# Norm factor moved behind the transposes: x is turned and split as it is, and the factor is applied to results and to a second pair of parts

## The chip, the core and the metric

One core of one Trainium2 chip runs the whole program. Its engines are TensorE (PE, with its weight loads as PEld), VectorE (DVE), ScalarE (ACT), GpSimd (POOL) and SyncE (SP, which here only issues DMAs). Each runs its own queue in order and waits on semaphores for the others. The metric is the device time of one execution in microseconds (us), the median of several runs. All times below are us unless marked ns.

## What is computed

A decoder trunk of two layers on 256 tokens of 1024 channels, in float32. Each layer has a mixer and a stage of experts, and each begins with an RMS norm:

```python
def rms_norm(x, g):
    y = x * lax.rsqrt(jnp.mean(x * x, axis=-1, keepdims=True) + EPS)
    return y * g

for layer in range(2):
    h = rms_norm(x, norm1_g[layer])
    dq, dk, dv, fq, fk, fv, ff, ga, gb = split(h @ w_in[layer])
    y_diff = diff_attention(dq, dk, dv, ...)          # 4 heads, softmax minus lambda softmax
    y_fox = forgetting_attention(fq, fk, fv, ff + b)  # 8 heads
    x = x + (sigmoid(ga) * (y_diff @ w_diff_o) + sigmoid(gb) * (y_fox @ w_fox_o)) @ w_out
    t = rms_norm(x, norm2_g[layer])
    s = product_keys(t @ w_query)                     # two top-16 of 128, then top 16 of their sums
    experts, gates = select(s)                        # softmax over the 16 best of each head
    x = x + sum(gates * gelu(t @ expert_u[experts]) * expert_v[experts])
return rms_norm(x, final_norm_g)
```

The norm is one factor per token (a row of x), times one gain per channel. All 16384 experts are computed densely, and a dense gate picks among them.

## The kernel before

Every product runs in three passes on PE. A float operand is split into a rounded part (`hi`) and the rest (`lo`), and hi by hi, hi by lo and lo by hi are added up in PSUM (`mm3`, `rows_b`). The activations' two parts are `hT[0]` and `hT[1]`, turned: channels on the partitions, in eight blocks k of 128, by 256 tokens.

Weights come as a list of blocks of 512 KB in a fixed order (`plan`): 8 of wV, 32 of wA, 8 of wO, 8 of w_out, 16 of wQ, 128 of uT and 128 of v in each layer. SP fetches a block into one of three buffers; ACT copies it rounded to `hi`, and DVE subtracts to get `lo` (lines 92 and 93), with three buffers of each. `weights` hands out block n and first calls `ahead(n + 3)`, so the instructions that split blocks n + 1 and n + 2 stand in the queues of ACT and DVE ahead of what the caller issues next. The order of the program is the order of each engine's queue (`manual_schedule`); nothing is reordered later.

Where a stage ends, `sum_b` adds products of rows into four PSUM banks (two halves of the tokens by two halves of the channels, `PIECES`). The last two blocks (`TAIL`) are kept back and run piece by piece, so that the pieces are done one after the other. `norm_t` follows: `inv_rms` adds each piece to x (DVE, line 210), squares it (ACT, line 216) and gets the factor by a power on POOL and a Newton step on DVE. A diagonal of factors is made for each half of the tokens, and PE multiplies blocks of x by it (line 248), which turns and scales x at once. ACT and DVE then write the two parts with the gain (lines 253 and 254).

In the mixer eight value blocks follow (wV, 18 matmuls each: two halves of the tokens, three passes, three column groups of 344). Between them stand small steps: the layer's constants and, behind the fourth block, two table loads of ACT (lines 386 and 387). Then come 32 projections on wA (`proj`, 24 matmuls of 256 columns each) with attention between them. In the experts' stage 16 projections on wQ give the queries; behind each stands the score product of the one before (`score`, which reads the copy `q`). Then 48 projections on uT run while DVE selects the experts: `select` is a generator whose items are placed into slots j = -13 to 47 by a budget of 1.35 for each slot (`PIECE_US`, the yields are its costs, None ends a slot). Behind slot 47 the generator is run to its end, the first one-hots are made (lines 749 and 751), and after one more projection PE makes the first dense gate from them (line 760).

## Time and profile before

| | |
|---|---|
| median of 3 runs | 2009.3 us (2009.29 to 2009.52) |
| the profiled execution | 2009.3 us, its span 2007.5 us |
| PE, PEld | 1992.8 us (99%), 1833.4 us (91%) |
| DVE, ACT, POOL | 1412.1 us (70%), 1058.8 us (53%), 27.4 us (1%) |
| PE's granted clock | 0.999 of full speed |
| DMA | 351.96 MB, 175 GB/s |

The page gives each engine's busy time and the chain of work that ended last, followed back from the last instruction. The views behind it list waits by engine and line, instructions in order of time with the idle time before each in brackets, groups of instructions by their shapes, and stretches of the span. PE's matmuls overlap: one that is listed with 0.40 us may be followed by the next after 0.23, so distances between starts are what PE takes.

### The profile page before, as it was taken

The page shows a single profiled execution, that of the slowest core. Times are in us where ns is not written, and L with a number is a line of the kernel's source. Part 1 is how long each engine was busy: PE and PEld are TensorE (multiplying, and loading weights), DVE is VectorE, ACT ScalarE, POOL GpSimd, SP SyncE. Part 2 cuts the span into 40 slices and gives each one's busy share as a digit, 9 for nine tenths or more (in the row PEclk, how much of TensorE's full clock was granted, in tenths as well). Part 3 has the DMA queues.
Part 4 walks back from the last instruction along what each step waited for, and adds up shares of the span by engine and source line. Part 5 has one row for each costly group of instructions (what it writes and reads, how often), then busy time and mean ns, then how long its engine had stood idle before and what let it go on. Part 6 is the DMA issues. An engine that isn't in the chain of part 4 may idle for free.

```text
span 2007.5 us, 35728 instructions
## 1 busy us (share of the span) xinstructions
PE 1992.8 (99%) x14042; PEld 1833.4 (91%) x14042; DVE 1412.1 (70%) x2867; ACT 1058.8 (53%) x1954; POOL 27.4 (1%) x49
## 2 busy tenths in 40 slices
PE   9999999999999999999999999999999999999998
PEld 8998999999999888888899989999999998888886
DVE  5667798788888555555566677987888885555555
ACT  6665556554444444444466655465444444444444
POOL 2000000000000000000010000000000000000000
PEclk9999999999999999999999999999999999999999
DMA  6445555555555555555554455565555555555554
GB/s 226 149 157 168 161 180 181 187 164 163 158 168 167 190 189 189 189 189 189 189 167 148 148 180 159 190 180 179 167 159 161 167 174 188 189 189 189 189 188 153
DMA packets 97451, 351.96 MB, mean 175 GB/s; under 512 B 11473, under 2 KB 11510, under 8 KB 97281
## 3 DMA queue, kind: packets, MB, share of 16 engines
q1 hardware_dynamic: 95040, 345.09, 54.5%
q0 software_dynamic: 1664, 3.53, 0.6%
q8 instruction: 110, 1.80, 0.4%
q10 hardware_dynamic: 576, 1.05, 0.1%
q14 instruction: 61, 0.49, 0.1%
HBM read 348.56 MB, written 1.71 MB: 174 GB/s over the span
## 4 chain that ended last, share of the span: by engine, by line
PE 99%; DVE 0%; DMA 0%; issue 0%; ACT 0%; POOL 0%; SPq 0%; ACTq 0%; DVEq 0%
PE acc L154 39%; PE ps L121 17%; PE ps L122 17%; PE ps L123 17%; PE acc L760 3%; PE ps L154 1%; PE acc L783 1%; PE acc L248 1%; PE acc L627 1%; PE ps L557 0%; PE acc L569 0%; PE acc L644 0%; DMA x<-x 0%; PE acc L122 0%; PE acc L123 0%
## 5 line engine op out<-in xcount | busy, mean ns | idle before, releaser
L93 DVE TENSOR_TENSOR lo<-raw,hi 128x1024 fp32r<-128x1024 f32 (+1 forms) x656 | 801.7, 1224 | 500.2 <-ACT hi L92 498.2
L92 ACT ACTIVATE hi<-raw 128x1024 fp32r<-128x1024 f32 (+1 forms) x656 | 694.4, 1059 | 396.3 <-PE acc L154 389.2
L121 PE MATMUL ps<-hT,hi 128*128 128x256 f32 x2784 | 794.6, 285 | 0.0
L122 PE MATMUL ps<-hT,hi 128*128 128x256 f32 x2784 | 784.6, 282 | 0.0
L123 PE MATMUL ps<-hT,lo 128*128 128x256 f32 x2784 | 778.9, 280 | 0.0
L154 PE MATMUL acc<-hi,cut 128*128 128x512 f32 x2048 | 561.1, 395 | 0.0
L121 PEld LDWEIGHTS ps<-hT,hi 128*128 128x128 f32 x2784 | 523.0, 188 | 3.9 <-issue 3.7
L123 PEld LDWEIGHTS ps<-hT,lo 128*128 128x128 f32 x2784 | 524.9, 189 | 0.0
L122 PEld LDWEIGHTS ps<-hT,hi 128*128 128x128 f32 x2784 | 523.4, 188 | 0.3
L154 PEld LDWEIGHTS acc<-hi,cut 128*128 128x128 f32 x2048 | 385.4, 188 | 90.0
L154 PE MATMUL acc<-lo,cut 128*128 128x512 f32 x1024 | 321.9, 394 | 0.0
L154 PEld LDWEIGHTS acc<-lo,cut 128*128 128x128 f32 x1024 | 192.4, 188 | 45.8
L730 ACT ACTIVATE g<-ps 128x8 f32<-128x8 f32 (+31 forms) x158 | 44.5, 282 | 265.3 <-PE ps L123 260.7
L675 ACT ACTIVATE bufa<-ps 128x256 f32<-128x256 f32 x96 | 36.9, 384 | 115.5 <-PE ps L123 115.5
L751 DVE TENSOR_TENSOR ohG<-oh,tT 128x2048 f16<-128x2048 f16 x64 | 78.4, 1225 | 2.2
L749 DVE TENSOR_TENSOR oh<-iotax,tT 128x2048 f16<-128x2048 f16 x64 | 77.8, 1216 | 0.0
L760 PE MATMUL acc<-ohG,oh 128*128 128x128 f16 x1024 | 70.0, 219 | 0.0
L701 DVE TENSOR_TENSOR cut<-bufb,cut 128x256 fp32r<-128x256 f32 x160 | 67.1, 419 | 0.0
L700 ACT ACTIVATE cut<-bufb 128x256 fp32r<-128x256 f32 x160 | 64.0, 400 | 0.0
L760 PEld LDWEIGHTS <-oh 128*128 128x128 f16 x1024 | 58.9, 97 | 2.9
L734 DVE TENSOR_TENSOR bufb<-bufb,g 128x8 f32<-128x8 f32 (+31 forms) x158 | 46.1, 292 | 15.3 <-ACT g L730 15.3
L772 DVE SCALAR_TENSOR_TENSOR bufa<-acc,bufa 128x192 f32<-128x192 f32 x128 | 44.8, 350 | 0.0
(231 smaller groups left out, 1383.9 us busy)
## 6 DMA issues: line engine op xcount, KB each, us to landing
raw<-uT SPq DMA_DIRECT2D x256, 512.0 KB, 3.7
raw<-expert_v SPq DMA_DIRECT2D x256, 512.0 KB, 3.6
raw<-wA SPq DMA_DIRECT2D x64, 512.0 KB, 3.6
raw<-wQ SPq DMA_DIRECT2D x32, 512.0 KB, 3.6
raw<-wV SPq DMA_DIRECT2D x16, 516.0 KB, 4.0
raw<-wO SPq DMA_DIRECT2D x16, 512.0 KB, 3.6
raw<-w_out SPq DMA_DIRECT2D x16, 512.0 KB, 4.4
tb<-table POOLq DMA_DIRECT2D x2, 640.0 KB, 6.1
```

What stands on the lines that cost most here:

```text
L92: nc.scalar.activation(hi[:, :w], raw[:, :w], AF.Copy)
L93: nc.vector.tensor_sub(lo[:, :w], raw[:, :w], hi[:, :w].bitcast(F32))
L121: self.nc.tensor.matmul(ps, ah, bh, start=first and q == 0, stop=False)
L122: self.nc.tensor.matmul(ps, ah, bl, start=False, stop=False)
L123: self.nc.tensor.matmul(ps, al, bh, start=False, stop=last and q == n - 1)
L154: self.nc.tensor.matmul(ps[:, :width], a, b[:, g * width:(g + 1) * width], start=first and n == 0, stop=last and n == 2)
L700: nc.scalar.activation(a[:, 0], chunk(n), AF.Copy)
L701: nc.vector.tensor_sub(a[:, 1], chunk(n), a[:, 0].bitcast(F32))
L734: nc.vector.tensor_mul(chunk(J)[:, :t0], chunk(J)[:, :t0], g[:, :t0])
L749: nc.vector.tensor_tensor(flat(oh), self.iotax.rearrange("p n t -> p (n t)")[:, None].to_broadcast([128, TB, 256]), cols[0][:, :, None].to ...
L751: nc.vector.tensor_tensor(flat(og), flat(oh)[:, None, TB * 128:].to_broadcast([128, 2, TB * 128]), cols[1][:, :, None].to_broadcast([128, ...
L760: self.nc.tensor.matmul(banks[t // 4][:, t % 4], oh[:, 0, t // 2, :, t % 2], og[:, k, t // 2, :, t % 2], start=k == 0, stop=k == 1)
```

## The change

`norm_t` is gone. Instead x is turned by PE transposes without the factor and split with the gain alone, a piece at a time (`tip`: four transposes of a piece and four ACT evictions; `turn_lo`: the DVE part). `sum_b` takes a target `turn` and puts the first three pieces' steps between its own last matmuls; the fourth (`turn_last`) stands inside the first product of the next stage. For layer 0's start three tips run at once.

The factor is computed beside the next stage by `scaled`, a generator of eight steps: squares, power, factor and diagonal, a product of a matrix of ones with the diagonals that spreads the factor over the partitions, and four steps that make a second pair of parts, two blocks k each (two DVE operations, an ACT copy, a DVE subtraction).

- Mixer: the value products use the unscaled `hT`; their results are scaled as they leave PSUM. The wA projections use the scaled pair `hs`. `scaled` takes one step behind each value block, two behind the seventh and eighth.
- Experts: `hs` holds the unscaled pair, on which all 16 query projections run; the factor enters the Exp of the gates. The scaled pair is written to `hT`, for uT. `scaled` takes steps in slots -15 to -12 and in -10, -8, -6 and -4; in these last four the selection gets no items.
- The first two query projections have an order of their own (`proj_first`): passes before blocks k.
- At the start all four x transfers go by SP's queue, and the identity by ACT's in place of POOL's.
- The order of k becomes 0 to 7, value banks are others, and `hs` lives in a pool that is opened for each layer and closed after the selection.

```diff
-KO = [0, 2, 4, 6, 1, 3, 5, 7]
+KO = list(range(KT))
...
+    def proj_first(self, h, *key, turn=False):
+
+        w = self.by_k(self.weights(*key))
+        ps = self.bank("ps")[:, :S]
+        lo, up = range(4), range(4, KT)
+        if turn:
+            order = [(0, 0, lo), None, (1, 0, lo), (0, 0, up), (1, 0, up), (0, 1, KO)]
+        else:
+            order = [(0, 0, KO), (0, 1, KO), (1, 0, KO)]
+        for n, o in enumerate(order):
+            if o is None:
+                self.turn_last()
+                continue
+            for k in o[2]:
+                self.nc.tensor.matmul(ps, w[o[0]][:, k], h[o[1]][:, k], start=n == 0 and k == 0,
+                                      stop=n == len(order) - 1 and k == KT - 1)
         return ps
...
-    def sum_b(self, n, key, lhs_of):
+    def sum_b(self, n, key, lhs_of, turn=None):
...
+        if turn:
+            self.turn_begin(*turn, [acc[1][0], acc[1][1]])
+        for p, (tt, c, width) in enumerate(PIECES):
             ps = acc[tt][c // 512][:, c % 512:c % 512 + width]
-            for lhs, w, j in late:
-                self.rows_b([ps], lhs, [p[:, c:] for p in w], tt, width, False, j == n - 1)
+            for m, (lhs, w, j) in enumerate(late):
+                last = turn and p == 3 and m == TAIL - 1
+                for n in range(3):
+                    if last and n == 2:
+                        self.tip(2)
+                    a = lhs[n // 2][..., tt * 128:(tt + 1) * 128]
+                    self.nc.tensor.matmul(ps, a, w[n % 2][:, c:c + width], start=False, stop=j == n_all and n == 2)
+                if turn and p == 2 and m == 0:
+                    self.tip(1)
+                    self.turn_lo(0, range(2))
             self.late.append(ps)
+            if turn:
+                if p < 3:
+                    self.add(p)
+                if p == 1:
+                    self.tip(0)
+                if p == 2:
+                    self.turn_lo(0, range(2, 4))
+                    self.turn_lo(1, range(2))
+                if p == 3:
+                    self.add(3)
+                    self.turn_lo(1, range(2, 4))
+                    self.turn_lo(2, range(4))
...
+    def tip(self, n):
...
+        for k in range(4):
+            nc.tensor.transpose(banks[n][:, k * 128:(k + 1) * 128],
+                                self.x[:, tt, c + k * 128:c + (k + 1) * 128], self.ident)
+        for k in range(4):
+            q = c // 128 + k
+            nc.scalar.activation(h[0][:, q, tt * 128:(tt + 1) * 128], banks[n][:, k * 128:(k + 1) * 128], AF.Copy,
+                                 scale=g[:, q:q + 1])
...
+    def turn_lo(self, n, ks):
...
+            self.nc.vector.scalar_tensor_tensor(h[1][:, q, tt * 128:(tt + 1) * 128], banks[n][:, k * 128:(k + 1) * 128],
+                                                g[:, q:q + 1], hv, op0=OP.mult, op1=OP.subtract)
...
+    def turn_last(self):
+        self.tip(3)
+        self.turn_lo(3, range(4))
+
+    def scaled(self, pool, h, out, rs):
...
+        for tt in range(2):
...
+            nc.scalar.activation(junk, self.x[:, tt], AF.Square, scale=1.0 / 32, accum_out=ss[:, tt:tt + 1])
+        yield
...
+        vy = self.rsqrt_begin(pool, v)
+        yield
...
+        for tt in range(2):
+            nc.vector.tensor_scalar(diag[:, tt], self.ident, rs[:, tt:tt + 1], None, op0=OP.mult)
+        yield
+        ps = self.bank("acc")[:, :S]
+        nc.tensor.matmul(ps, self.ones, diag.rearrange("p t c -> p (t c)"), start=True, stop=True)
+        rb = self.ring(pool, "rb", [128, S], F32, 1)
+        nc.scalar.activation(rb, ps, AF.Copy)
+        yield
+        for k in range(0, KT, 2):
+            t = self.ring(pool, "nt", [128, 2, S], F32, 1)
+            ks = slice(k, k + 2)
+            nc.vector.tensor_add(t, h[0][:, ks].bitcast(F32), h[1][:, ks].bitcast(F32))
+            nc.vector.tensor_tensor(t, t, rb[:, None, :].to_broadcast([128, 2, S]), op=OP.mult)
+            nc.scalar.activation(out[0][:, ks], t, AF.Copy)
+            nc.vector.tensor_sub(out[1][:, ks], t, out[0][:, ks].bitcast(F32))
+            yield
...
-                    eng = nc.scalar if tt else nc.sync
-                    eng.dma_start(self.x[:, tt, cs], i["x"][0, tt * 128:(tt + 1) * 128, cs])
+                    nc.sync.dma_start(self.x[:, tt, cs], i["x"][0, tt * 128:(tt + 1) * 128, cs])
             self.ident = const.tile([128, 128], F32, name="ident")
-            nc.gpsimd.dma_start(self.ident, i["c_ident"])
+            nc.scalar.dma_start(self.ident, i["c_ident"])
...
-            self.norm_t(ap, self.gains[:, 0, l])
+            if l == 0:
+                self.turn_begin(self.hT, self.gains[:, 0, l], [self.bank("acc") for _ in range(2)])
+                for n in range(3):
+                    self.tip(n)
+                    self.turn_lo(n, range(4))
+            rs = self.rs[0]
+            sc = self.scaled(ap, self.hT, self.hs, rs)
...
                 for tt in range(2):
                     self.rows_b(psv[tt], (self.hT[0][:, k], self.hT[1][:, k]), w, tt, WV, n == 0, n == KT - 1)
+                    if n == 0 and tt == 0:
+                        self.turn_last()
+                next(sc, None)
+                if n >= 6:
+                    next(sc, None)
...
-                        ps = self.proj("wA", l, 4 * q + c, tag="acc" if c == 0 and q < 2 else "ps")
+                        ps = self.proj(self.hs, "wA", l, 4 * q + c, tag="acc" if c == 0 and q < 2 else "ps")
...
-                    ps = self.proj("wQ", l, j + 16) if j < 0 else self.proj("uT", l, j)
+                    if j < -14:
+                        ps = self.proj_first(self.hs, "wQ", l, j + 16, turn=j == -16)
+                    else:
+                        ps = self.proj(self.hs, "wQ", l, j + 16) if j < 0 else self.proj(self.hT, "uT", l, j)
+                    if -15 <= j <= -12 or j in (-10, -8, -6, -4):
+                        next(sc, None)
...
-                    if j >= -13:
+                    if j >= -13 and j not in (-10, -8, -6, -4):
```

## Rows read from the trace of the kernel before

**Rows 1.** The page, parts 1 and 4: busy time; the chain by engine.

```profile
PE 1992.8 (99%) x14042; PEld 1833.4 (91%) x14042; DVE 1412.1 (70%) x2867; ACT 1058.8 (53%) x1954; POOL 27.4 (1%) x49
...
PE 99%; DVE 0%; DMA 0%; issue 0%; ACT 0%; POOL 0%; SPq 0%; ACTq 0%; DVEq 0%
```

**Rows 2.** Waits of PE, whole span: us in total, times, longest.

```profile
PE acc L248 <- DVE diag L245: 3.3, 2, 2.2
PE acc L248 <- issue: 2.7, 2, 1.3
```

**Rows 3.** Timeline, mixer to experts, layer 0: start, us, instruction [idle before].

```profile
189.46 1.23 DVE L93 TENSOR_TENSOR lo<-raw,hi 128x1024 fp32r<-128x1024 f32 x1 [1.57 <-ACT hi L92]
...
190.60 1.28 DVE L210 TENSOR_TENSOR x<-acc,x 128x512 f32<-128x512 f32 x2
...
193.47 0.40 PE L154 MATMUL acc<-hi,mT 128*128 128x512 f32 x1
...
193.91 0.69 DVE L210 TENSOR_TENSOR x<-acc,x 128x512 f32<-128x512 f32 x1
...
195.19 3.99 PE L248 MATMUL acc<-diag,x 128*128 128x128 f32 x32 [1.32 <-issue]
...
198.94 0.36 PE L121 MATMUL ps<-hT,hi 128*128 128x256 f32 x1
...
202.24 0.28 PE L121 MATMUL ps<-hT,hi 128*128 128x256 f32 x1
```

**Rows 4.** Timeline, experts of layer 0 to mixer of layer 1.

```profile
1003.75 0.40 PE L154 MATMUL acc<-hi,cut 128*128 128x512 f32 x1
...
1009.14 0.72 PE L154 MATMUL ps<-hi,hT 128*128 128x344 f32 x3
...
1012.53 0.64 PE L154 MATMUL ps<-hi,hT 128*128 128x344 f32 x3
...
1015.37 0.63 PE L154 MATMUL ps<-hi,hT 128*128 128x344 f32 x3
```

**Rows 5.** Chain that ended last, in order of time: start, us, what.

```profile
44.97 0.43 PE acc L522 x2
...
52.34 0.33 PE ps L557 x3
...
391.47 0.94 PE acc L760 x16
```

**Rows 6.** Timeline, start of the program.

```profile
1.93 0.56 POOL L283 DMA_DIRECT2D gains<-norm_g  x1
...
15.53 0.64 PE L154 MATMUL ps<-hi,hT 128*128 128x344 f32 x3
```

**Rows 7.** DMA issues, 0 to 40 us: queue, count, KB, us to landing.

```profile
gains<-norm_g POOLq DMA_DIRECT2D x1, 16.0 KB, 5.7
```

**Rows 8.** Stretch 5 to 10 us: busy (count) by engine, clock, DMA, GB/s.

```profile
5.00:10.00 5.00, 2.82 (x25) 2.63 (x25) 2.04 (x9) 4.29 (x10) 2.26 (x5) 1.00 0.91 357
```

**Rows 9.** Groups by line and shape: busy us, mean ns of one, idle before.

```profile
L92 ACT ACTIVATE hi<-raw 128x1024 fp32r<-128x1024 f32 x640 | 677.3, 1059 | 384.3 <-PE acc L154 380.6 <-DMA raw<-wA 2.7 <-ACT gates L484 0.7
...
L254 DVE SCALAR_TENSOR_TENSOR hT<-acc,gains,hT 128x256 fp32r<-128x256 f32 x32 | 13.4, 478 | 0.8 <-ACT hT L253 0.8
L253 ACT ACTIVATE hT<-acc,gains 128x256 fp32r<-128x256 f32 x32 | 13.1, 477 | 5.6 <-PE acc L248 5.6
```

**Rows 10.** Timeline of ACT, value blocks of layer 1.

```profile
1019.48 1.28 ACT L386 ACT_TABLE_LOAD   x1
...
1022.40 1.05 ACT L92 ACTIVATE hi<-raw 128x1032 fp32r<-128x1032 f32 x1
```

**Rows 11.** Timeline of DVE, selection and first one-hot, layer 0.

```profile
211.77 0.48 DVE L793 MAX8 tv<-s 128x8 f32<-128x128 f32 x2
...
214.11 1.21 DVE L93 TENSOR_TENSOR lo<-raw,hi 128x1024 fp32r<-128x1024 f32 x1
...
388.35 1.22 DVE L749 TENSOR_TENSOR oh<-iotax,tT 128x2048 f16<-128x2048 f16 x1
```

More of the change, by code (lines that the diff above doesn't have):

```diff
@@ L235, in inv_rms, with add @@
         yield next(end)
-    def norm_t(self, pool, g):
-        nc = self.nc
-        inv = self.inv_rms()
-        banks = None
-        for tt in range(2):
-            diag = self.ring(pool, "diag", [128, 128], F32, 2)
-            nc.vector.tensor_scalar(diag, self.ident, next(inv), -0.5, op0=OP.mult, op1=OP.mult)
-            banks = banks or [self.bank("acc").rearrange("p (k t) -> p k t", k=2) for _ in range(4)]
-            for k in range(KT):
-                nc.tensor.matmul(banks[k // 2][:, k % 2, tt * 128:(tt + 1) * 128],
-                                 self.x[:, tt, k * 128:(k + 1) * 128], diag, start=True, stop=True)
-        self.ahead(self.used + 2)
-        for k in KO:
-            ps = banks[k // 2][:, k % 2]
-            nc.scalar.activation(self.hT[0][:, k], ps, AF.Copy, scale=g[:, k:k + 1])
-            nc.vector.scalar_tensor_tensor(self.hT[1][:, k], ps, g[:, k:k + 1], self.hT[0][:, k].bitcast(F32),
-                                           op0=OP.mult, op1=OP.subtract)
+    def add(self, n):
+        tt, c, width = PIECES[n]
+        xv = self.x[:, tt, c:c + width]
+        self.nc.vector.tensor_add(xv, self.late[n], xv)
@@ L293, in build @@
             for l in range(self.depth):
-                self.mixer(l)
-                self.peer(l)
+                with ExitStack() as hu:
+                    hp = hu.enter_context(tc.tile_pool(name="hu", bufs=1, side="right"))
+                    self.hs = [hp.tile([128, KT, S], F32R, name=f"hs{q}") for q in range(2)]
+                    self.rs = [hp.tile([128, 2], F32, name=f"rs{q}") for q in range(2)]
+                    self.mixer(l)
+                    self.peer(l, hu)
             with tc.tile_pool(name="fin", bufs=1) as fin:
@@ L898, in select @@
         yield None
-        nc.scalar.activation(e, e, AF.Exp)
+        for tt in both:
+            hs = slice(tt * PH, (tt + 1) * PH)
+            nc.scalar.activation(e[:, hs], e[:, hs], AF.Exp, scale=self.rs[1][:, tt:tt + 1])
         halve(8)
```

60 lines of the change are left out of this document (40 added, 20 removed).

## The prediction, made before the result

> **What bounds the kernel now.** The page first: PE is busy 99% of the span and the chain that ended last is 99% PE [rows 1]. So only PE's own work and PE's idle time count, and the waits of PE come next: 6.0 us of the idle time stand at the transposes of line 248 [rows 2]. A wait shows only a part, so the third view is the timeline at the boundaries. Mixer to experts, layer 0: the last matmul of the sum starts at 193.47 and, 0.23 each, is through at 193.70; the next projection starts at 198.94 and the one behind it at 202.24 [rows 3]. So 8.54 us go by for one projection, which takes 2.82 elsewhere (24 matmuls, 0.1175 apart): 5.7 too many, 4.0 of them line 248's 32 passes. Experts to mixer: through at 1003.98, first value block at 1009.14, second at 1012.53, and a block is 2.84 [rows 4]; again 5.7 too many. There are three such boundaries, and a start whose second block begins at 15.53 [rows 6].
>
> The view by groups has the prices of ACT and DVE. They bound nothing now, but every block of weights needs one ACT copy (`hi`, 1.06) and then one DVE subtraction (`lo`, 1.23, the next operation 1.14 behind it) in a fixed order [rows 3, 9].
>
> Prices: a float transpose is 0.11 (three in 0.33); the `ones` product is 0.43, as line 522's, of the same size [rows 5]. An eviction of 128x256 is 0.48 on ACT and on DVE [rows 9]. Half that size isn't shown in this use: between 0.24 and 0.48; I take 0.30 apart on ACT and 0.285 on DVE, near the half, since instructions on one engine overlap by some 0.07. A DVE operation on 128x512 floats lasts 0.69, an unrelated one may follow after 0.60 (two in 1.28) [rows 3]; an ACT copy of that size I take at 0.62, from `hi`'s 1.06 for twice the elements less a fixed part (0.53 to 0.69). Another engine sees PE's result 0.2 after the matmul is through (193.70 to 193.91) [rows 3].
>
> **The change, part by part.** I set each queue out in program order, each instruction when its engine and its operands are ready.
>
> *Boundary to the experts (two).* Removed: the wait for the norm and the two-pass products. Added: 16 transposes. Twelve stand inside the sum's tail, 1.32; the first also waits for the first addition, which stands behind the `lo` of the next weights [rows 3], 0.4. So the sum is through 1.7 later. Then DVE sets the end, for its queue holds: the last addition (0.2 + 0.60), six `turn_lo` (1.7), the `lo` of two blocks (2.28), which `weights` issues ahead of `turn_last`, and four `turn_lo` (1.14). That is 5.9, with the last matmul and its waits 6.3. Total 8.0 for 8.54: 0.5 saved, not 5.7. ACT's queue is alike: three tips, two `hi`, then the last tip.
>
> *Boundary to the mixer of layer 1.* The same 1.7, then nine matmuls, four transposes, nine matmuls (0.157 each): 3.27. The second block begins 5.0 after the old end of the sum, before it was 8.55. Nothing late stands in front, as blocks 1 to 3 need only the first tips: 3.6 saved.
>
> *Start.* Evictions now need the gains. Their DMA took 5.7 from an issue at 1.93 [rows 6, 7]; now first on POOL's queue, at about 1.2, it lands at some 6.5 (5.5 to 7.5). Twelve evictions end at 10.1, the first `hi` at 11.2, its `lo` at 12.4; 15 matmuls and four transposes later the second block begins at 15.3, for 15.53: 0.2 saved (1.2 to -0.8). The x and ident transfers move too (x on SP alone, two issues more ahead of the first weights there; ident on ACT's queue): covered by the gains' later landing; without that cover 0.9, two issues.
>
> *The factor.* Four `ones` products on PE: 1.7 in all, uncovered.
>
> *The second pair of parts in the mixers (two): the costly step.* It is off PE, but in the ACT and DVE queues of `hi` and `lo`, and the first projection on wA needs its last quarter. Count from the start of the fifth value block. ACT has waited for the `ones` product, which stands behind the fourth block on PE; then come its eviction (0.2 + 0.3) and the table loads of lines 386 and 387 with their operations (2.9, from 1019.48 to 1022.40 [rows 10]), which before ran beside the fourth block. ACT is free at 3.4; before it was at 1.4 (1022.40 against 1012.53 + 3 x 2.84 [rows 4, 10]). From there each step is a ring through two engines: `hi` 1.06, `lo` 1.14, addition 0.73, product 0.72, copy 0.53, and only then the next `hi`. That is 4.2, where PE's block is 2.84. So `hi` begins at 3.4, 7.6 and 11.8, and the lead of two blocks is eaten. Behind the third `hi` come two quarters: their copies begin at 15.5 and 18.2, the last subtraction ends at 19.5, and PE ends its first projection at 20.1; without a wait it would at 4 x 2.83 + 2.82 = 14.1. So 6.0 are lost, and 0.6 at the next projection, whose `hi` and `lo` stand behind the last quarter: 6.6 in each mixer. Bounds: 4, if the engines hand over at once and the lead is longer; 9, if the late evictions also hold up attention.
>
> *The same in the experts' stage (two).* A quarter in every second projection; a projection with its score is 3.27. In the seven concerned DVE has 7 x 1.14 of `lo`, four quarters at 2.7 (0.65 of each a wait for ACT) and two items of selection at 2.34 (211.77 to 214.11, [rows 11]): 23.5 in 22.9, besides waits for `hi`. ACT stands until a quarter's product is there, and the copy of `q` that PE's score needs is queued behind. Set out in order, three scores wait 1.2, 0.3 and 0.8: 2.3 in each layer, from 0 to 4.
>
> *Selection skips four slots.* Counting its yields, it ended in slot 44 of 47 before; four slots later its last transposes stand in slot 47 and the last evictions behind them. The first one-hot (388.35) then begins 1.6 later against the same point of PE; the pair, 1.22 and as much again, ended 0.65 ahead of the dense product at 391.47 [rows 5, 11]. So 1.0 is lost in each layer, 0 to 1.5.
>
> *At nothing:* scales on evictions already made, another order of k, one more Exp, fewer powers on POOL: ACT and DVE hide them; uncovered, under 0.5 in all.
>
> **Sum.** Saved 2 x 0.5 + 3.6 + 0.2 = 4.8. Lost 1.7 + 2 x 6.6 + 2 x 2.3 + 2 x 1.0 = 21.5. Net 16.7 on the profiled execution's 2009.3 (its span is 2007.5), which is also the median of the runs: 2026.0 us.
>
> **The clock.** PE's granted clock is 1.00 in the stretch from 5 to 10 us, where PE is busy 2.82 of 5 [rows 8]; the new waits come in pieces of at most 1.4, so I leave the clock at 2.4 GHz. The Trainium skill, "TensorE: Matmul & The Clock Gate", section "HAM oscillation — how this bites in real kernels", says that gaps in PE's work let its clock fall back to the lower level, 1.2 GHz. By that rule the matmuls behind a stalled projection would run slower; no row here is at that level. Rival 3 is that case: if in each mixer one or two projections of 2.82 took twice as long, 3 to 6 us in each would come on top, 2032 to 2038.
>
> **Rivals.**
> 1. The lead holds: ACT is idle 1.8 of each 2.84 block, and the quarters fit in. Against it: the ring's length counts, not the engines' load; it decides at a ring of 2.84. Then no stall is left: 2009.3 - 4.8 + 1.7 = 2006.2, with the selection's 2.0 2008.2. As 4.0 us (0.2%) is about what a measurement of this kernel can tell from no change, that is mostly "same"; it is faster only if the gains land early too (2005).
> 2. Only the mixers stall; experts and selection are covered: 2009.3 - 4.8 + 1.7 + 13.2 = 2019.4.
> 3. The clock falls: 2035.
> 4. The transposes aren't shorter than the products: the tail grows by 0.25 - 0.11 for each of 64, 9 us more. Line 557's row speaks against it [rows 5]; under 0.02, so it stands in no range.
>
> **How the numbers follow.** Forecast with all three losses 0.55; rival 2 0.20; rival 1 0.18, of which same 0.12 and faster 0.06; rival 3, or a stall that spreads into attention, 0.07. The bounds of the unknown prices (mixers 8 to 18, experts 0 to 8, selection 0 to 3, start 1 either way) reach from 2013 to 2034 around the forecast and rival 2; leaving out rival 1 and the top: 2012 to 2032. Faster 0.06, same 0.13, slower 0.81.
>
> **What will show it.** Right: PE waits of 0.6 to 1.4 in the first wA projection, ended by ACT and DVE on `hs`; `hi` copies 4.2 apart in the value blocks; layer 1's second value block 5.0 after the old end of the sum; the first wQ projection waiting for `turn_lo`; scores waiting for `q`; the dense product waiting for the one-hots. Wrong: a first wA projection of 2.8 without a wait, or `hi` copies that keep 2.84. The likeliest single error is the size of the mixers' stall.

## The result and the profile after

The changed kernel takes 2035.4 us (median of 4 runs, 2033.6 to 2035.9) for 2009.3 before: ratio 1.0128, 95% interval 1.0115 to 1.0141. It is 26.1 us slower; the forecast was 16.7, and 2032 was the top of its range. The profiled execution has a span of 2034.1 (before 2007.5), mean granted clock 0.995.

The page of after, parts 1 and 4 (the lines that answer to [rows 1]):

```profile
PE 2002.4 (98%) x13986; PEld 1835.3 (90%) x13986; DVE 1445.9 (71%) x2943; ACT 1071.3 (53%) x1992; POOL 26.3 (1%) x44
...
PE 38%; DVE 1%; ACT 1%; issue 0%; ACTq 0%
```

The chain through PE was 99% before; followed back now it accounts for some 40% of the span, so waits and timelines have to tell the rest. Waits of PE in after (us in total, times, longest), where [rows 2] had two of line 248:

```profile
PE acc L172 <- ACT hi L92: 5.0, 3, 4.6
PE acc L121 <- ACT hs L341: 3.6, 4, 1.3
PE acc L894 <- ACT q L783: 3.0, 4, 1.0
PE ps L146 <- ACT hs L294: 2.2, 4, 0.9
PE acc L871 <- DVE ohG L862: 2.1, 2, 1.1
PE acc L123 <- DVE lo L93: 1.5, 2, 0.8
...
PE acc L332 <- DVE diag L329: 0.7, 1, 0.7
```

Five of these stand in the forecast: the second pair (L341), the scores (L894), the last tip (L146, where the forecast had DVE's `turn_lo` in place of ACT's evictions), the one-hots (L871) and the late `lo` (L123). Two do not: 4.6 us in one piece ahead of the first value block, and the `ones` product's wait for `diag`.

How far after is behind, from PE's timeline at the same work (start before, start after), with what each step lost and what the forecast had for it:

| point | before | after | behind | lost here | forecast |
|---|---|---|---|---|---|
| second value block, layer 0 | 15.53 | 20.15 | 4.6 | +4.6 | -0.2 |
| forget's product, layer 0 (L522, now L627) | 44.81 | 57.87 | 13.1 | +8.4 | +7.0 |
| first score product | 205.07 | 217.31 | 12.2 | -0.8 | -0.5 |
| first dense product | 391.31 | 407.47 | 16.2 | +3.9 | +3.7 |
| second value block, layer 1 | 1012.53 | 1025.22 | 12.7 | -3.5 | -3.6 |
| forget's product, layer 1 | 1040.88 | 1063.85 | 23.0 | +10.3 | +7.0 |
| first score product | 1201.09 | 1223.37 | 22.3 | -0.7 | -0.5 |
| first dense product | 1387.38 | 1413.52 | 26.1 | +3.9 | +3.7 |
| end of the span | 2007.5 | 2034.1 | 26.6 | +0.5 | 0 |

The forecast column takes the prediction's terms, 0.43 of each `ones` product among them. Six of the nine steps are right within 0.5. The start is off by 4.8, and the mixers by 1.4 and 3.3. The experiments take these up in turn, and then the terms that came out right.

The granted clock (the last number but two) in after, by stretches:

```profile
10.00:15.00 5.00, 0.86 (x3) 0.79 (x3) 2.58 (x9) 1.83 (x5) 0.51 (x1) 0.76 0.72 273
15.00:20.00 5.00, 4.96 (x21) 4.53 (x19) 3.25 (x5) 3.66 (x7) 0.00 (x0) 0.56 0.64 202
...
45.00:50.00 5.00, 2.52 (x15) 1.71 (x14) 3.36 (x5) 2.16 (x4) 0.00 (x0) 1.00 0.31 107
50.00:55.00 5.00, 5.00 (x29) 4.86 (x30) 4.35 (x11) 4.26 (x9) 0.00 (x0) 0.66 0.49 159
...
1050.00:1055.00 5.00, 2.76 (x15) 1.85 (x13) 3.47 (x6) 2.02 (x3) 0.00 (x0) 0.87 0.36 105
1055.00:1060.00 5.00, 4.98 (x23) 4.98 (x24) 4.36 (x11) 4.27 (x8) 0.00 (x0) 0.50 0.44 149
```

It falls three times, each time in or behind a stretch in which PE waits much: at the start and in the first wA projection of each mixer. A mean of 0.50 means the lower level, 1.2 GHz, for the whole stretch. PE counts as busy there, so the busy share hides the loss; the number of its instructions shows it, 23 matmuls where an undisturbed stretch of such projections has 42.

### The profile page after: what moved, and what is told of

It reads as the page before. It is cut to its first block, busy times and chain, and to the rows that moved or that the text cites. A ratio compares the mean times of both kernels' runs of the same rounds, so it can differ in the third digit from the quotient of the medians.

```text
span 2034.1 us, 35698 instructions
## 1 busy us (share of the span) xinstructions
PE 2002.4 (98%) x13986; PEld 1835.3 (90%) x13986; DVE 1445.9 (71%) x2943; ACT 1071.3 (53%) x1992; POOL 26.3 (1%) x44
## 5 line engine op out<-in xcount | busy, mean ns | idle before, releaser
L121 PE MATMUL ps<-hT,hi 128*128 128x256 f32 x2048 | 580.7, 284 | 0.0
L122 PE MATMUL ps<-hT,hi 128*128 128x256 f32 x2048 | 576.6, 282 | 0.0
L123 PE MATMUL ps<-hT,lo 128*128 128x256 f32 x2048 | 572.9, 280 | 0.0
L172 PE MATMUL acc<-hi,cut 128*128 128x512 f32 x2016 | 551.1, 395 | 0.0
L123 PEld LDWEIGHTS ps<-hT,lo 128*128 128x128 f32 x2048 | 386.1, 189 | 0.0
L122 PEld LDWEIGHTS ps<-hT,hi 128*128 128x128 f32 x2048 | 384.8, 188 | 0.0
L121 PEld LDWEIGHTS ps<-hT,hi 128*128 128x128 f32 x2048 | 384.6, 188 | 0.0
L172 PE MATMUL acc<-lo,cut 128*128 128x512 f32 x1008 | 315.6, 394 | 0.0
L121 PE MATMUL ps<-hs,hi 128*128 128x256 f32 x704 | 204.7, 291 | 0.0
L122 PE MATMUL ps<-hs,hi 128*128 128x256 f32 x704 | 198.2, 282 | 0.0
L123 PE MATMUL ps<-hs,lo 128*128 128x256 f32 x704 | 197.0, 280 | 0.0
L121 PEld LDWEIGHTS ps<-hs,hi 128*128 128x128 f32 x704 | 132.3, 188 | 3.9 <-issue 3.7
L123 PEld LDWEIGHTS ps<-hs,lo 128*128 128x128 f32 x704 | 132.7, 189 | 0.0
L122 PEld LDWEIGHTS ps<-hs,hi 128*128 128x128 f32 x704 | 132.5, 188 | 0.2
```

Source lines behind the costliest of these rows:

```text
L121: self.nc.tensor.matmul(ps, ah, bh, start=first and q == 0, stop=False)
L122: self.nc.tensor.matmul(ps, ah, bl, start=False, stop=False)
L123: self.nc.tensor.matmul(ps, al, bh, start=False, stop=last and q == n - 1)
L172: self.nc.tensor.matmul(ps[:, :width], a, b[:, g * width:(g + 1) * width], start=first and n == 0, stop=last and n == 2)
```

## The experiments

Theory: (a) the mixers' stall is a ring through ACT and DVE, 4.2 us per block, and not their load; (b) behind the stalls PE's clock falls, which costs more on top; (c) the start is late because POOL's constant transfers moved ahead of the weights. Rivals stand with each run. Where a mixer's loss is measured, the yardstick is the distance from the start of the fifth value block to the first logits product: 20.57 before (24.98 to 45.55 in layer 0), 28.78 and 29.61 after.

### The start

Before, POOL's powers for the norm waited for the squares, and eight constant transfers stood behind them. POOL's timeline before:

```profile
6.77 0.56 POOL L182 TENSOR_TENSOR rs_y<-rs_v,mhalf 128x1 f32<-128x1 f32 x1 [4.28 <-DVE rs_v L223]
...
8.81 0.59 POOL L354 DMA_DIRECT2D bf<-b_forget  x1
...
12.57 0.55 POOL L327 DMA_DIRECT2D oh<-c_bucket  x1
```

and after, where nothing holds them, with what ACT waits for meanwhile:

```profile
1.94 0.56 POOL L451 DMA_DIRECT2D bf<-b_forget  x1
...
6.03 0.55 POOL L418 DMA_DIRECT2D oh<-c_bucket  x1 [0.35 <-DMA gains<-norm_g]
```

```profile
5.82 1.28 ACT L294 ACT_TABLE_LOAD   x1 [5.82 <-DMA gains<-norm_g]
...
13.03 1.06 ACT L92 ACTIVATE hi<-raw 128x1032 fp32r<-128x1032 f32 x1 [2.34 <-DMA raw<-wV]
```

ACT is free for the first `hi` at 10.7 and waits 2.34 for its block of weights.

**pool_late** puts the transfers behind a late result again:

```diff
+            if l == 0:
+                nc.gpsimd.tensor_tensor(self.const.tile([128, 1], F32, name="gate"), self.hT[1][:, 3, 128:129].bitcast(F32),
+                                        self.mhalf[:, 0:1], op=OP.add)
             bf = mp.tile([128, 8], F32, name="bf")
```

> The changed kernel, but at layer 0 POOL's eight constant transfers stand behind a small POOL addition that reads a result of the third early tip's subtraction (about 9.5 us), as the power that waited for the squares held them back before. Theory (these transfers, issued at 1.9 to 6.0 us instead of 8.8 to 12.6, take the DMA engines from x and from the first wV blocks, and PE's granted clock falls in the wait that follows): the first hi copy no longer waits 2.3 us for its raw block, the second value block begins at 15.3 (20.15 in the changed kernel), the clock is 1.00 from 10 to 20 us, and the time is 2035.4 - 4.8 = 2030.6 (2029.6 to 2031.6). Rival (x on SP's queue alone and the first weights issued 0.94 us later are the cause): at most 1 us is won, 2034.4 to 2035.4, and the raw block still lands at 13.0.

Measured: 2033.1 us (ratio 1.0119, 1.0102 to 1.0135), 2.3 less than after, where 4.8 was expected. Its PE timeline and its stretches:

```profile
11.99 0.58 PE L172 MATMUL acc<-hi,hT 128*128 128x344 f32 x2 [3.38 <-ACT hi L92]
...
13.61 0.73 PE L172 MATMUL acc<-lo,hT 128*128 128x344 f32 x2 [0.88 <-DVE lo L93]
...
18.07 0.48 PE L172 MATMUL acc<-hi,hT 128*128 128x344 f32 x2
```

```profile
10.00:15.00 5.00, 2.14 (x9) 1.85 (x10) 4.89 (x14) 3.84 (x7) 2.77 (x6) 0.89 0.05 5
15.00:20.00 5.00, 5.00 (x28) 4.94 (x28) 1.96 (x5) 3.39 (x9) 2.21 (x5) 0.77 0.83 257
```

The weights are no longer late: the first `hi` starts at 10.79, right behind the evictions, and the second block begins at 18.07 instead of 20.15. So 2.1 of the 4.6 are the transfers, and the rival is out. The cause is surer than its size: the seven kernels here that issue the transfers as after does (after, filler, no_pair_mixer, no_pair_experts, tables, no_ring, piece) begin the second block at 18.95 to 20.41, 0.9 to 2.3 later than this one, and in each of them the first `hi` waits 1.6 to 3.3 for its weights. But the clock still falls, for PE still has 3.38 to wait; expecting it at 1.00 was wrong. The rest is found in the kernel called best, below: with products that nobody reads in that wait, the clock is 1.00 and the second block begins at 16.59, so 1.5 is the clock. What is left of the 4.6, 1.1, stands in front of the first block: ACT's evictions ahead of `hi`, and 0.88 until DVE has `lo`.

**two_queues** also undoes the other move of the start:

```diff
-                    nc.sync.dma_start(self.x[:, tt, cs], i["x"][0, tt * 128:(tt + 1) * 128, cs])
+                    eng = nc.scalar if tt else nc.sync
+                    eng.dma_start(self.x[:, tt, cs], i["x"][0, tt * 128:(tt + 1) * 128, cs])
-            nc.scalar.dma_start(self.ident, i["c_ident"])
+            nc.gpsimd.dma_start(self.ident, i["c_ident"])
```

> The kernel with POOL's constant transfers held back, and besides x on SP's and ACT's queue and ident on POOL's, as before the change. Theory (the moved queues of x and ident cost nothing, since the twelve evictions set the first hi): the first weights are issued 0.94 earlier, but the first hi still begins when ACT is through with the evictions, at 10.8, or later, since the gains now stand behind ident on POOL; 2033 to 2034. Rival (they are part of the start's loss): hi begins 0.9 earlier and the second block at 17.2 instead of 18.07, 2032.2.

Measured in one run: 2034.9, span 2033.0 (pool_late 2031.6). From its timelines of ACT and PE:

```profile
7.89 1.28 ACT L294 ACT_TABLE_LOAD   x1 [7.89 <-DMA gains<-norm_g]
```

```profile
13.39 0.94 PE L172 MATMUL acc<-hi,hT 128*128 128x344 f32 x2 [5.51 <-ACT hi L92]
```

The gains land at 7.89 instead of 5.21 (pool_late), and the first block begins at 13.39 instead of 11.99. The weights are issued 0.94 sooner, but no `hi` starts sooner for it, since ACT's evictions come last, here as in pool_late. So the rival is out, and the gains, first on POOL's queue, are worth 1.4 by this one run.

### The clock behind the mixers' stalls

**filler** gives PE work in the place of waits:

```diff
             self.ahead(self.used + 3)
+            fill = self.bank("acc")[:, :S]
+            for _ in range(32):
+                nc.tensor.matmul(fill, self.hT[0][:, 0, 0:128], self.hT[0][:, 0], start=True, stop=True)
```

> The changed kernel with 32 products of 128x256 whose result nobody reads, 3.76 us of PE's time, between the eighth value block and the first wA projection of each mixer, in the place of waits. Theory (the stall ends when the last quarter is ready, and behind it PE runs at 1.2 GHz for 3.5 us in layer 0 and 6 us in layer 1, which costs 1.6 and 2.4 us): the last quarter is ready at the same point, the granted clock stays near 1.00 behind it, and the time falls by 4.0 to 2031.4 (2030.4 to 2032.4), although 7.5 us of work were added. Rival 1 (the lower clock has another cause than PE's waits): the clock is 0.5 to 0.7 as before and the time stays within 1 us of 2035.4. Rival 2 (the stall is not a wait for the quarters, which the extra work could stand in for): slower by up to 7.5, 2043.

Measured: 2032.5 us (1.0116, 1.0099 to 1.0133): 2.9 less than after, where 4.0 was expected, with 64 products more. Stretches of filler behind the stalls, where after has 0.66 and 0.50:

```profile
50.00:55.00 5.00, 4.59 (x40) 4.40 (x39) 4.14 (x14) 4.26 (x10) 0.00 (x0) 1.00 0.57 189
...
1055.00:1060.00 5.00, 5.00 (x44) 5.00 (x44) 3.85 (x17) 4.26 (x10) 0.00 (x0) 1.00 0.66 209
```

The yardstick falls to 27.79 and 27.82: 1.0 and 1.8 less. So the fall of the clock comes from PE's waits, and both rivals are out. By the distances of matmuls in after (0.214 instead of 0.1175), the lower level cost 1.5 in layer 0 (15 matmuls from 50.24) and 2.4 in layer 1 (25 from 1055.02). Not all of that comes back, since the second projection, now sooner there, waits 0.4 for DVE's `lo`.

### The ring in the mixers

In after, the `hi` copies start at 33.53, 37.74 and 41.97, that is 4.2 apart, from 3.7 behind the fifth block (29.83) on. PE's timeline of its first wA projection:

```profile
46.31 0.39 PE L121 MATMUL acc<-hs,hi 128*128 128x256 f32 x1 [0.55 <-ACT hs L341]
47.03 0.39 PE L122 MATMUL acc<-hs,hi 128*128 128x256 f32 x1 [0.34 <-DVE hs L342]
...
49.15 0.39 PE L121 MATMUL acc<-hs,hi 128*128 128x256 f32 x1 [1.26 <-ACT hs L341]
49.87 0.38 PE L122 MATMUL acc<-hs,hi 128*128 128x256 f32 x1 [0.34 <-DVE hs L342]
...
50.46 0.42 PE L122 MATMUL acc<-hs,hi 128*128 128x256 f32 x1
```

PE waits for each quarter, first for ACT's copy and then for DVE's subtraction; in the last row the clock has fallen.

**no_pair_mixer** leaves the quarters out:

```diff
-                next(sc, None)
-                if n >= 6:
-                    next(sc, None)
+                if n < 4:
+                    next(sc, None)
...
-                        ps = self.proj(self.hs, "wA", l, 4 * q + c, tag="acc" if c == 0 and q < 2 else "ps")
+                        ps = self.proj(self.hT, "wA", l, 4 * q + c, tag="acc" if c == 0 and q < 2 else "ps")
...
```

> The changed kernel without the second pair of parts in the mixers: squares, power, diag and the ones product stay, the four quarters are left out, and the wA projections read the first pair, so the norm's factor is missing from them. Theory (ring of five steps, 4.2 us each, costs 6.6 us in each mixer, and the fall of the clock behind it 1.6 and 2.4): 2035.4 - 13.2 - 4.0 = 2018.2 (2017 to 2019.5), first wA projection 2.8 us without a wait, clock 1.00. Rival 1 (the clock falls for another reason): 2022.2, with the lower clock still there. Rival 2 (the table loads or the late ones product stall the value blocks by themselves): waits for hi and lo stay in the blocks and more than 2024 is left.

Measured: 2019.0 us (1.0048, 1.0031 to 1.0065), 16.4 less than after. The yardstick is 20.76 in both layers, the clock 1.00, and no wait on `hi`, `lo` or `hs` is left in the mixers. So the table loads and the late `ones` product alone stall nothing (rival 2 is out), and all of the mixers' loss hangs on the quarters. This does not yet tell order from load.

**tables** moves the table loads one block ahead:

```diff
-                if n == 3:
+                if n == 2:
                     nc.vector.tensor_scalar(gsub, gsub, -0.5 * (1.0 - lam_init), None, op0=OP.mult)
...
-                if n == 4:
+                if n == 3:
                     nc.vector.tensor_sub(nlam, ls[:, 1:2], ls[:, 0:1])
```

> The changed kernel with the step that makes the mixers' lambda constant (two table loads with their operations, 2.9 us of ACT) one value block earlier, ahead of the ones product instead of behind it. Theory (what counts is when the ring of 4.2 us starts): hi begins 0.5 after the start of the fifth block instead of 3.4, the ring keeps its 4.2, and the stall ahead of the third wA projection falls by 2.9 in each mixer: 2035.4 - 5.8 = 2029.6, and down to 2025.6 if the shorter stall leaves the clock at its upper level. Rival (ACT is not what the ring waits for at its start; the ones product or DVE is): hi copies begin where they did, 2034.5 to 2036.

Measured: 2030.6 us (1.0105, 1.0089 to 1.0120), 4.8 less than after; 5.8 was expected. ACT's timeline in layer 0 (the fifth block starts at 28.89):

```profile
29.55 1.06 ACT L92 ACTIVATE hi<-raw 128x1032 fp32r<-128x1032 f32 x1
...
33.78 1.05 ACT L92 ACTIVATE hi<-raw 128x1032 fp32r<-128x1032 f32 x1
...
38.00 1.05 ACT L92 ACTIVATE hi<-raw 128x1024 fp32r<-128x1024 f32 x1
```

The ring starts 0.7 behind the fifth block instead of 3.7 and keeps its 4.2: as the theory says. The yardstick falls by 2.05 and 2.2, less than 3.0. In layer 0 the clock takes the rest back: by the distances it is low for 26 matmuls instead of 15, which costs 1.0 more. In layer 1 the ring starts 1.3 behind the fifth block, not 0.7. The stretches of layer 0, in which PE has no wait before 42 us:

```profile
35.00:40.00 5.00, 5.00 (x34) 5.00 (x33) 4.00 (x5) 1.59 (x2) 0.00 (x0) 1.00 0.75 253
40.00:45.00 5.00, 3.21 (x22) 2.61 (x20) 3.68 (x6) 1.12 (x2) 2.00 (x3) 0.99 0.56 191
45.00:50.00 5.00, 4.66 (x20) 4.37 (x21) 4.32 (x10) 4.27 (x9) 0.00 (x0) 0.50 0.50 176
```

**no_ring** keeps all the work and changes the order (with tables' edit, and a second buffer `nt` that the order needs):

```diff
-            t = self.ring(pool, "nt", [128, 2, S], F32, 1)
+            t = self.ring(pool, "nt", [128, 2, S], F32, 2)
...
             nc.vector.tensor_tensor(t, t, rb[:, None, :].to_broadcast([128, 2, S]), op=OP.mult)
+            yield
             nc.scalar.activation(out[0][:, ks], t, AF.Copy)
             nc.vector.tensor_sub(out[1][:, ks], t, out[0][:, ks].bitcast(F32))
-            yield
+        yield
...
-                if n >= 6:
+                if n in (3, 6):
                     next(sc, None)
...
-                    if -15 <= j <= -12 or j in (-10, -8, -6, -4):
+                    if -15 <= j <= -12 or j in (-10, -8, -6, -4, -2):
```

> The changed kernel with the same work in another order: the table loads one block earlier, and each quarter in two steps, so that the ACT copy and the last subtraction of a quarter are issued behind the next block's hi and lo, and beside the addition and product of the next quarter (two nt buffers; first step in the fourth block, last in the seventh; in the experts' stage five slots instead of four). Theory (the stall is the ring through ACT and DVE, not their load: 8 quarters' operations of 2.13 and three lo of 1.15 are 12.0 us on DVE, and 12.9 pass from the factor to the last quarter's first use): no wait on hs is left, the third wA projection starts 17.0 after the fifth block, the clock stays at 1.00, and in the experts' stage the scores' waits go: 2035.4 - 16.4 - 4.5 = 2014.5 (2013 to 2017). Rival (DVE's load is too high in whatever order): hs or lo waits of 2 to 5 us stay in each mixer, 2022 to 2030.

Measured: 2016.1 us (1.0033, 1.0021 to 1.0045), 19.4 less than after. The yardstick is 20.76 in layer 0, the same as without any quarters, and 22.52 in layer 1, where these waits are left:

```profile
PE acc L123 <- DVE lo L93: 0.4, 1, 0.4
PE acc L122 <- DVE hs L343: 0.3, 1, 0.3
PE acc L121 <- ACT hs L342: 0.2, 1, 0.2
```

The same operations, and no stall in layer 0: it was the order. The rest in layer 1 begins with the wait for `diag`, which has another cause (below, best2).

### The experts' stage

**no_pair_experts** leaves the quarters out there:

```diff
-                    if -15 <= j <= -12 or j in (-10, -8, -6, -4):
+                    if -15 <= j <= -12:
```

> The changed kernel without the second pair in the experts' stage: the ones product stays, the four quarters are left out, and the projections on uT read what is left in the first pair's tiles, so their input is not this layer's; the selection still skips its four slots. Theory (ACT stands for each quarter's product with the copy of q queued behind it; the selection ends late because of the skipped slots): the scores' waits go, 1.5 to 2.3 us in each layer, and the dense products still wait about 1.0 each: 2030.8 to 2032.4. Rival 1 (the one-hots are late because the quarters load DVE, not because of the skipped slots): their waits go as well, 2028.8 to 2030.4. Rival 2 (the scores wait for the selection's own work): 2034.5 to 2035.5.

Measured: 2030.1 us (1.0106, 1.0089 to 1.0123). From the first score to the first dense product it is 187.91 in layer 0 (215.69 to 403.60), for 190.16 in after and 186.24 before; in layer 1 187.90 for 190.15. So the quarters cost 2.25 in each layer, and the waits on `q` are gone. The dense products still wait:

```profile
PE acc L871 <- DVE ohG L862: 2.1, 2, 1.1
```

so the quarters' load is not what makes the one-hots late (rival 1 is out). The time fell by 5.3, 0.8 more than twice 2.25; in its profiled execution the fifth block of layer 0 begins 1.2 sooner than in after and the mixers' distances are 0.4 and 0.6 shorter. The remainder lies there, where how long the clock stays low differs from run to run.

**piece** lets the selection catch up:

```diff
-PIECE_US = 1.35
+PIECE_US = 1.5
```

> The changed kernel with 1.5 us of selection work handed out in each slot instead of 1.35, so that the selection makes up for its four skipped slots. Theory (the one-hots are late because the selection ends late): the dense products' waits of 1.05 in each layer go, 2035.4 - 2.1 = 2033.3, or down to 2032.7 with the 0.3 that a waiting product needs to start again. Rival (the selection's later part, or the eviction of its last transposes, is late whatever its pace): waits stay, 2035 to 2036; or more work in each slot makes lo late and PE wait, over 2036.

Measured: 2032.0 us (1.0114, 1.0098 to 1.0129). No wait of the dense product is left, and from score to dense product it takes 188.92 and 188.99, 1.2 less in each layer than after. The skipped slots were the cause. The time fell by 3.5; the 1.1 beyond these 2.4 is again in the second mixer.

### All remedies together

**best**: pool_late, no_ring and piece, and 14 products in PE's wait at the start.

```diff
+                for _ in range(14):
+                    nc.tensor.matmul(self.turning[2][3][:, 0:128], self.ones, self.ones, start=True, stop=True)
             rs = self.rs[0]
```

> All four remedies in one kernel: POOL's constant transfers behind the third tip, 14 products of 128x128 that nobody reads in PE's wait at the start, the order of the kernel without the ring, and 1.5 us of selection in each slot. Theory, from the runs so far: 2035.4 - 2.3 (start, measured) - 1.5 (start's clock, estimate) - 16.4 (mixers, as measured without the pair) - 4.5 (experts' quarters, as measured without them) - 2.1 (selection) = 2008.6 (2007 to 2011), that is, level with the kernel before: what the change saves at the boundaries (0.8 + 0.8 + 3.4) goes for the four ones products, the diag wait and the start. Rival (the remedies get in each other's way: selection at 1.5 and quarters both load DVE): 2012 to 2016.

Measured: 2013.0 us (1.0017, 1.0008 to 1.0026), 4.4 above the theory. The start is as expected (clock 1.00, second block at 16.59), but the gains do not add up: from the fifth block (26.87) to the first logits product layer 0 takes 23.1, where no_ring takes 20.76. The late start had given ACT and DVE a lead over PE, as I read it: in best the fifth block begins 3.2 earlier than in no_ring (30.10), and the late transfers are in front: the constants' product waits 0.50 for its transfer, and lambda's exponential on ACT 0.84 for DVE, with `hi` and `rb` behind it.

**best2** takes up what best shows.

```diff
+        if turn:
...
+            w = self.by_k(self.split[self.used])
+            self.used += 1
...
                 self.turn_last()
+                self.ahead(self.used + 2)
...
-                for n in range(3):
+                for n in (0, 2):
                     self.tip(n)
...
-                if n == 2:
+                if n == 3:
                     next(const, None)
...
-            nc.gpsimd.memset(fq[1][0:64], 0.0)
-            nc.gpsimd.memset(fk[1][0:64], 0.0)
+            for t in (fq[1], fk[1]):
+                t = t[0:64].rearrange("p k t -> p (k t)")
+                nc.scalar.activation(t, self.x[0:64, 0, :t.shape[1]], AF.Copy, scale=0.0)
```

> The kernel with all four remedies (2013.0 us) and five more moves. At the start only the tips that the first value block reads are turned ahead of it, the third tip behind its first half (estimate from the rows: eight evictions instead of twelve ahead of the first hi, the first block 1.1 earlier); the constants' second step is one block later, where its transfer has landed (0.5 of wait and what it costs to start again, 0.8, and lambda's operations no longer hold ACT up, 0.8); the two zero fills go from POOL to ACT, since in layer 1 the 128x2 operation that makes rs took 1.38 us on DVE beside POOL's fill and 0.17 in layer 0 without one (0.75 of diag wait, and a ring that starts 1.2 later); and at the boundary to the experts the last tip is issued ahead of the next two blocks' hi and lo instead of behind them (ACT stands 2.0 in hi ahead of it; 1.1 in each layer). Theory: 2013.0 - 1.1 - 1.6 - 0.75 - 1.2 - 2.2 = 2006.2 (2005 to 2008.5), below the kernel before; rs takes 0.2 in layer 1 and no diag wait is left. Rival for rs (DVE's operation is long for another reason): it stays at 1.4 and 2 us less are won. Rival for the boundary (the last addition on DVE sets its end): nothing is won there, 2008.4.

Measured: 2010.9 us (1.0008, 0.9999 to 1.0017). Some of its parts hold. The second block begins at 15.90 instead of 16.59, 0.7 of the 1.1 expected. The last tip ahead of the weights' `hi` and `lo` brings PE's waits on it at line 146 from 2.2 to 0.4, and from forget's product to the first score product it takes 158.34 in layer 1 instead of best's 159.46. And `rs`: DVE's timeline of after, layers 0 and 1,

```profile
26.01 0.17 DVE L326 TENSOR_SCALAR rs<-rs_y 128x2 f32<-128x2 f32 x1
...
1032.68 1.38 DVE L326 TENSOR_SCALAR rs<-rs_y 128x2 f32<-128x2 f32 x1
```

POOL's timeline of after,

```profile
1032.60 0.97 POOL L501 MEMSET fq<- 64x1024 f32 x1
1033.49 0.54 POOL L502 MEMSET fk<- 64x512 f32 x1
```

and the same operation of best2 in layer 1, without fills on POOL:

```profile
1019.64 0.17 DVE L332 TENSOR_SCALAR rs<-rs_y 128x2 f32<-128x2 f32 x1
```

In after it ends with POOL's second fill (1034.06 and 1034.03). The rival for `rs` is out. But 4.7 of the expected 6.8 did not come: on ACT the fills (1.04 and 0.62) stand ahead of forget's exponential, and forget's product waits 0.94 and 0.65 for `nls`; in layer 0 the `ones` product now waits 0.56 for `diag`. Waits were moved.

**best3** and **best4**: the fills are POOL's again, behind an operation that reads `diag`; the two transfers of the constants' product go ahead of most others on POOL; lambda's step is one block earlier (best3) and then split, its loads where best2 has them (best4):

```diff
+            nc.gpsimd.tensor_tensor(mp.tile([128, 1], F32, name="gate2"), self.diag[:, 1, 0:1], self.mhalf[:, 0:1], op=OP.add)
             nc.gpsimd.memset(fq[1][0:64], 0.0)
...
-                if n == 3:
+                if n == 1:
                     nc.vector.tensor_scalar(gsub, gsub, -0.5 * (1.0 - lam_init), None, op0=OP.mult)
...
+                if n == 2:
                     nc.scalar.activation(nlam, self.mhalf[:, 0:1], AF.Ln, scale=-2.0)
                     nc.scalar.activation(ls, ls, AF.Exp)
```

> The kernel of 2010.9 us with its new waits taken out: the zero fills are POOL's again, but behind a small POOL addition that reads diag, so that they can't stand beside the operation that makes rs (on ACT they held forget's chain, 0.94 and 0.65 of wait at its product); lambda's step is one more block earlier, so that ACT no longer stands in front of rb for it (the ring's first hi and rb begin 0.7 to 1.0 earlier, and the last quarter's waits of 0.34 and 0.39, with what it costs to start again 1.3 in each mixer, go or shrink); and the two transfers of the constants' product go ahead of the others on POOL, its small DVE operations behind lambda's. Theory: 2010.9 - 1.6 - 2 x 1.0 - 0.5 = 2006.8 (2005.5 to 2008.5), below the kernel before. Rival (DVE's load in the mixers, 12.0 of 12.9 us, leaves the last quarter late wherever the ring begins): waits on hs of 0.3 to 0.4 stay, 2008.5 to 2010.

Measured: 2007.8 us (0.9992, 0.9983 to 1.0001): the waits on `hs` are gone, but the table loads, now ahead of a `hi`, make `diag` late (waits of 1.62 and 0.42).

> The kernel of 2007.8 us with lambda's step cut in two: its small DVE operations stay in the second value block, its two table loads with their operations on ACT go back to the third. Theory (in that kernel the loads stood ahead of a hi, its lo ahead of rs and diag, and the ones product waited 1.62 and 0.42 for diag): the diag waits go, 2.0 and what it costs to start again, and the ring of quarters begins no later, since exp no longer waits for DVE: 2007.8 - 2.0 = 2005.8 (2005 to 2007), ratio 0.998. Rival (hi, now ahead of the loads, only passes the wait on to rb and the quarters): waits on hs come in their place, 2007 to 2008.5.

Measured: 2005.2 us (0.9979, 0.9970 to 0.9988), 4.3 below the kernel before, and the only version here whose interval lies below 1 (best3's reaches 1.0001). All of its waits of 0.4 or more:

```profile
PE ps L384 <- DVE ones L381: 1.1, 1, 1.1
PE acc L178 <- DVE lo L93: 0.9, 1, 0.9
PE ps L296 <- DVE x L283: 0.7, 3, 0.2
PE ps L152 <- ACT hs L300: 0.4, 2, 0.2
PE acc L123 <- DVE lo L93: 0.4, 1, 0.4
```

The yardstick is 20.77 and 21.67. So the change gains only when its side work is off PE's path. How much of the 4.3 is its own these runs don't tell: moves that it doesn't need, such as those of lambda's step, were not tried on the kernel before.

## Why the prediction was wrong, and where it was right

The sign was right, the size 9.4 us too small, and the time lies above the range. The range is also cut lower than its own bounds: above the forecast they are 4.8 for the mixers, 3.4 for the experts, 1.0 for the selection and 1.0 for the start, together 2036.2, where the prediction writes 2034. That would have held the time, but not for the reasons below.

**What bounds the kernel, and the boundaries: right in size, with the wrong engine named.** 0.8 and 0.7 were saved at the two boundaries to the experts (0.5 forecast) and 3.5 at the mixer of layer 1 (3.6). But the prediction lets DVE set the end at the experts and has the first wQ projection wait for `turn_lo`; no such wait came. PE waits there for ACT's evictions (L294), 0.23 and 0.86 in layer 0. The prediction called ACT's queue alike, so the size came out by both counts. best2 won 1.1 by taking the weights' `hi` and `lo` out of the way of both engines.

**The ring: right to a few tenths.** Forecast 4.2 for each turn, from 3.4 behind the fifth block on, and 6.6 lost. Measured: 4.2, from 3.7 on, and 8.2 and 9.0 lost, of which 1.5 and 2.4 are the clock: 6.7 and 6.6. no_ring shows that the order is the cause, as rival 1's counterargument said (the ring's length counts, not the load).

**Experts and selection: right.** 2.3 forecast and 2.25 measured for the quarters, in two waits on `q` in each layer, not three; 1.0 forecast, and a wait of 1.05, with its restart 1.2, measured for the selection.

**The clock: wrong.** The step that failed is the sentence that leaves it at 2.4 GHz, from one stretch of [rows 8] and the length of single waits. In that row PE is busy 2.82 of 5 without a fall; in tables it is busier, 3.21 of 5 with 5.00 before it, and the next stretch is at 0.50. So one row without a fall is no bound. Nor is the length of single waits: in both mixers of after none was longer than 1.26. Rival 3 named this case, with a chance of 0.07 and 3 to 6 us for each mixer; it came, at 1.5 and 2.4, and also at the start (1.5), which the rival did not look at. The rule that the prediction cited (the Trainium skill, "TensorE: Matmul & The Clock Gate", section "HAM oscillation — how this bites in real kernels": gaps in PE's work let its clock fall back) agrees with these rows in its direction; its example is one long wait in each turn of a loop, and here short ones were enough. It deserved more weight than the one row that was set against it.

**The start: wrong.** Forecast 0.2 saved, measured 4.6 lost. The step that failed is "fewer powers on POOL" among the edits at nothing. The power was counted as work that goes, not as what eight transfers stood behind. Without it they are issued at 1.94 to 6.03 instead of 8.81 to 12.57, and the first weights land late: 2.1 by pool_late. 1.5 more is the clock. The last 1.1 is a mis-sized term: `hi` was expected at 10.1 and can start at 10.7, and DVE's `lo` comes 0.9 after PE wants it. That the moved queues of x and the identity are covered was right (two_queues).

**The wait for diag: missed.** 0.75 in layer 1, for POOL's two fills stood beside the small DVE operation that makes `rs`; this too is a step that moved past work on POOL.

Together: 16.7 forecast, 4.8 for the start, 3.9 for the clock in the mixers and 0.8 for `diag` make 26.2, for 26.1 measured. That the start and the clock add up so closely is partly luck, since how long the clock stays low differs by a microsecond between runs, and the start by 1.5.

## What to carry to other kernels

When an edit removes an operation that waits, look at what stood behind it in its queue: transfers that were held back by it start earlier and may take the DMA engines from what the first product needs. Side work that is split over two engines in turns costs the length of the ring, not its load. Issue each step one block behind the one that it waits for: here the same operations then cost 0.2 in layer 0 (20.76 for 20.57) instead of 8.2. Where PE's waits follow each other closely, price the lower clock behind them as a term of its own, and read it from the granted clock and from the count of matmuls in a stretch, since the busy share doesn't show it.

## What the runs showed of the hardware

The granted clock fell behind waits of which none was longer than 1.3 us (0.66 and 0.50 in the two mixers), and products without a reader in their place kept it at 1.00 (filler, best). In layer 0 of tables three waits, 0.37, 0.34 and 1.27, were enough. Which length or number of waits decides, these runs don't tell.

A DVE operation on 128x2 elements took 1.38 us instead of 0.17 while POOL filled two tiles, and it ended with the second fill. A two-source subtraction did not: in best3 a fill begins at 1020.19, and DVE's timeline is

```profile
1020.15 1.23 DVE L93 TENSOR_TENSOR lo<-raw,hi 128x1032 fp32r<-128x1032 f32 x1
1021.30 0.69 DVE L346 TENSOR_TENSOR nt<-hT,hT 128x512 f32<-128x512 f32 x1
```

that is, 1.15 for the subtraction as elsewhere. The Trainium skill, "SBUF — State Buffer", section "SBUF: two separate sides", says that DVE and POOL share one pair of ports, which one of them holds for a whole instruction while the other stands still, and that DVE takes part in this in a mode that uses two ports, and with two sources in SBUF only against a POOL operation that reads SBUF. The rows agree in which operation waits and which does not; whether the small one ran in such a mode, and why it waited for the second fill too, they don't show.

Eight transfers by POOL's queue, 0.4 MB together, took 7.6 to 10.6 us each when they were issued beside x and the weights. From 5 to 10 us the DMA engines moved 175 GB/s, for 357 in [rows 8] and 346 in pool_late.
